# A transformer layer on one core: the residual stream by tokens instead of by features

## The chip, the cores and the metric

The kernel runs on one core of one Trainium2 chip. The metric is the device time of one execution in microseconds. The core has five engines that work side by side: TensorE (PE, the matrix products; its weight loads stand apart as PEld), VectorE (DVE), ScalarE (ACT), GpSimd (POOL) and SyncE (SP, here only the queue of most transfers). A matrix product contracts over the 128 partitions: one operand stands still in the array (the stationary one, up to 128 columns), the other moves through it (up to 512 columns), and the result lands in a bank of PSUM with the stationary operand's columns as its partitions. Everything else works on SBUF or PSUM, 128 partitions at a time.

## The reference

One layer on 512 tokens of width 1024, in fp32. The attention part (two kinds of sparse attention, merged by two sigmoid gates) gives `merged`; the change begins behind it:

```
x = x + merged @ w_out[i]
gate, up = jnp.split(rms_norm(x, g_ffn[i]) @ w_ffn_in[i], 2, axis=-1)
x = x + (jax.nn.silu(gate) * up) @ w_ffn_out[i]
ple_gate = jax.nn.sigmoid(rms_norm(x, g_ple[i]) @ w_ple_gate[i])
x = x + ple_gate * (p[i] @ w_ple_proj[i])
```

`rms_norm` divides each token by the root of the mean square of its 1024 features and multiplies by a gain per feature. The FFN's hidden width is 2816, or 22 tiles of 128. `p` has 512 tokens of width 256.

## The kernel before

**Products.** Every fp32 operand is split into a high and a low part in the matmul's format: ACT copies the high part (`wh`, `x2h`), DVE subtracts it for the low one (`wl`, `x2l`). A product is three matmuls: high by high, high by low, low by high. In `tmm` (L467) the weights stand still and the activations, kept transposed (features on partitions, 512 tokens along the row), move; results come out transposed too.

**The stream.** From the output projection on the residual stream X2 is kept transposed, eight tiles of 128 features by 512 tokens. `w_out` (`wob`, L470-472) makes one feature tile after the other, 24 matmuls each; `residual` (L1066) adds half of it to X2 on DVE, splits it with the gain (L338 on ACT, L339 on DVE) and adds its square to `ssum` (ACT, then POOL). The norm of a token is a sum over partitions, so `rms_stats` (L430) takes it on PE: eight small matmuls with ones (L434, `st1b`), the power -0.5 on POOL (L438), and eight products with a diagonal that spread it over the partitions (L445, `st1c`) into `rb`. It is multiplied in behind the first FFN product.

**The FFN.** The hidden width goes by 22 tiles `m`. The first six are plain (`hidden_plain`): gate `fg` and up `fu`, 24 matmuls of 512 columns each. The others (`hidden_seven`, `seven`) use seven block products in the place of eight, in banks `sa`, `sb`, `sc`, 84 matmuls of 256 columns a tile; the sums of weight blocks that these need are made by POOL's queue with transfers that add in memory (`adding`, L259, two steps of `add` for each pair of blocks and sum), and those of the activations by `normed_blocks` and `Blocks` on DVE. The output product runs three times (`ffn_out`, behind tiles 8, 16 and 21), also by seven block products, with the hidden tiles standing still; so its results have tokens on the partitions. They gather in `acc` (`xn`), added by `into` from banks on DVE (in phase 0 most are first written by copies on ACT).

**The end.** The embedding product (`pj`, 48 matmuls in `pjb`, L1279) stands ahead of the last `ffn_out`. In `turned_back` (L1322) 32 transposes on PE (L1324, `fob`) turn `acc` round, DVE adds X2 (read back from memory, where `kept` holds it since L1298), ACT and DVE split it, and the squares are summed. The gate product (`pg`, 8 output tiles in `pgb`) begins with three tiles on the first four feature tiles, goes on when the upper four are split, and `gated` (L1352) multiplies by `rb2`, takes the tanh, multiplies with the embedding, adds X2 and writes the transposed output, which the host turns.

**Order.** Weights are loaded by SP in the order of a list `units`, into buffers of two tags, `wr` (three) and `wx` (two, L80: the first block "11" of `ffn_out` and half the blocks of a seven-product tile), up to seven ahead, and split into four `wh` and `wl`; each get of one splits the one after next (L128). The instructions are ordered per engine before the run by a scheduler that simulates them; `tc.issue_after` binds one behind another. Engines then run their queues strictly in order.

Of the kernel before, what the change touches and what calls it, by code (L numbers as in the profile page):

```python
# [18 lines left out]
S = 512  # L19
# [6 lines left out]
PLAIN = 6  # L26
# [6 lines left out]
BIG_BUFS = 33  # L33
# [5 lines left out]
OUT_ORDER = [("11", 0), ("11", 1), ("t1", 0), ("t2", 0), ("t1", 1), ("t2", 1), ("21", 0), ("22", 0)]  # L39
OUT_LATE = [[("t3", 0), ("t3", 1), ("21", 1), ("22", 1), ("t4", 0), ("t4", 1)],  # L40
            [("21", 1), ("22", 1), ("t3", 0), ("t3", 1), ("t4", 0), ("t4", 1)]]
# [19 lines left out]
class Weights:  # L61
# [11 lines left out]
    def load(self, upto):  # L73
        while self.n_raw < min(upto, len(self.units)):
# [5 lines left out]
            pool, bufs = (self.pool, 3) if tag == "wr" else (self.more, 2)  # L80
# [20 lines left out]
    def parts(self):  # L101
# [9 lines left out]
        if tag != "wr" and key[0] == "fo":  # L111
            self.kept[key[3]] = t
# [7 lines left out]
        for a, b in self.pieces(i, n):  # L120
            for c, d in self.halves(i, n) if i else [(a, b)]:
                self.nc.scalar.activation(h[:, c:d], t[:, c:d], AF.Copy)  # L122
# [84 lines left out]
def hybrid_kernel(ctx: ExitStack, tc: tile.TileContext, a, out):  # L207
# [45 lines left out]
    for nm, c in (("un", 4), ("wo", 8)):  # L253
        units += [((nm, i), a[nm][i], 1024) for i in range(c)]
# [4 lines left out]
    def adding():  # L259
# [20 lines left out]
        for m in range(0, a["fi7"].shape[2], 4):  # L280
            yield from pair_of_sums(a["fi7"], m, 4, put_fi)
# [20 lines left out]
    def out_units(ph):  # L302

        for name, kp in OUT_ORDER + OUT_LATE[ph == 2]:
# [5 lines left out]
                   "t2": lambda: f"11{kp}", "22": lambda: f"11{kp}"}[name]()  # L310
            yield (("fo", ph, name, f"{name}{kp}"), src, n, "wx" if name == "11" else "wr")
# [28 lines left out]

    ssum = cp.tile([128, 512], F32, name="ssum")

    def add_square(src, first):
        if first:
            A.activation(ssum, src, AF.Square)
        else:
            q = t2("sqx")
            A.activation(q, src, AF.Square)  # L348
            G.tensor_tensor(ssum, ssum, q, op=OP.add)  # L349
# [40 lines left out]
    big_mask = cp.tile([128, 512], F32, name="big_mask")  # L390
# [39 lines left out]
    def rms_stats(name, tags="ss", sums=None):  # L430
        if sums is None:
            sums = bank(name + "b", tags[0])[:, :QT]
            for i in range(QT):
# [1025 lines left out]
```

## Time and profile before

| | us |
|---|---|
| median of 3 runs | 840.03 |
| lowest, highest | 835.34, 840.16 |
| the profiled execution | 834.49 |
| its span | 832.6 |
| PE busy | 815.4 (98%) |
| DVE, ACT, POOL busy | 651.0, 479.6, 173.5 |
| output projection from, to | 384.22, 428.26 |
| plain FFN tiles to | 495.40 |
| last matmul | 827.29 |

The span is that of the profiled instructions; the execution's own time lies 1.9 us above it. In rows of a timeline the first number is the start in the span, the second the duration, then the engine, the line, the result and its sources, and in brackets the idle time of the engine before it with what ended it. Matmuls are pipelined: their durations overlap, so a stage is read from start to start.

### The profile page before, as it was taken

The page shows a single profiled execution, that of the slowest core. Times are in us where ns is not written, and L with a number is a line of the kernel's source. Part 1 is how long each engine was busy: PE and PEld are TensorE (multiplying, and loading weights), DVE is VectorE, ACT ScalarE, POOL GpSimd, SP SyncE. Part 2 cuts the span into 40 slices and gives each one's busy share as a digit, 9 for nine tenths or more (in the row PEclk, how much of TensorE's full clock was granted, in tenths as well). Part 3 has the DMA queues.
Part 4 walks back from the last instruction along what each step waited for, and adds up shares of the span by engine and source line. Part 5 has one row for each costly group of instructions (what it writes and reads, how often), then busy time and mean ns, then how long its engine had stood idle before and what let it go on. Part 6 is the DMA issues. An engine that isn't in the chain of part 4 may idle for free.

```text
span 832.6 us, 12780 instructions
## 1 busy us (share of the span) xinstructions
PE 815.4 (98%) x4653; PEld 712.2 (86%) x4653; DVE 651.0 (78%) x1175; ACT 479.6 (58%) x899; POOL 173.5 (21%) x203
## 2 busy tenths in 40 slices
PE   9999999999999999999999999999999999999897
PEld 8888898788788888787888889789999889988786
DVE  7799677888787987749637988777888977967955
ACT  6455655967676767733433546545666446664531
POOL 3726244010000110106322242000111100200211
PEclk9999999999999999999999999999999999999999
DMA  9443554488664776735442347344445354544402
GB/s 340 145 123 117 154 148 154 127 206 217 187 175 112 203 190 176 184 98 201 165 141 83 106 122 201 113 150 138 138 129 177 100 149 119 153 146 148 149 26 101
DMA packets 39981, 125.13 MB, mean 150 GB/s; under 512 B 5104, under 2 KB 5488, under 8 KB 36464
## 3 DMA queue, kind: packets, MB, share of 16 engines
q1 hardware_dynamic: 34448, 91.82, 34.3%
q0 software_dynamic: 3968, 28.31, 14.3%
q10 hardware_dynamic: 1504, 4.21, 1.6%
q8 instruction: 36, 0.59, 0.3%
q14 instruction: 25, 0.20, 0.1%
HBM read 116.98 MB, written 32.51 MB: 180 GB/s over the span
## 4 chain that ended last, share of the span: by engine, by line
PE 86%; DVE 9%; ACT 2%; issue 1%; DMA 1%; POOL 0%; DVEq 0%; ACTq 0%; POOLq 0%
PE sa L470 4%; PE sa L472 3%; PE sa L471 3%; DVE wl L125 3%; PE ga L470 3%; PE pt L914 3%; PE ga L471 3%; PE ga L472 3%; PE sv L1266 2%; PE sv L1269 2%; PE sv L1268 2%; PE sc L470 2%; PE sc L471 2%; PE sc L472 2%; PE wob L471 2%; PE pv L938 2%
## 5 line engine op out<-in xcount | busy, mean ns | idle before, releaser
L122 ACT ACTIVATE wh<-wr 128x512 fp32r<-128x512 f32 (+2 forms) x243 | 196.2, 828 | 193.8 <-issue 37.4
L125 DVE TENSOR_TENSOR wl<-wr,wh 128x1024 fp32r<-128x1024 f32 (+2 forms) x195 | 229.4, 1180 | 70.7 <-ACT wh L122 69.9
L470 PE MATMUL ga<-xh,wh 128*128 128x512 f32 x128 | 53.5, 418 | 0.0
L889 DVE CUSTOM_DVE_ANT_0 p<-sb,big_mask 128x512 f32<-128x512 f32 (+2 forms) x96 | 44.4, 484 | 9.8 <-PE sb L887 9.5
L471 PE MATMUL ga<-xl,wh 128*128 128x512 f32 x128 | 50.4, 394 | 0.0
L472 PE MATMUL ga<-xh,wl 128*128 128x512 f32 x128 | 50.4, 393 | 0.0
L914 PE MATMUL pt<-ident,p 128*128 128x128 f32 x240 | 38.7, 274 | 1.5 <-DVE pw L924 1.5
L924 DVE TENSOR_TENSOR pw<-pt,pw 128x512 fp32r<-128x512 f32 x48 | 32.6, 683 | 6.0 <-ACT pw L923 5.7
L923 ACT ACTIVATE pw<-pt 128x512 fp32r<-128x512 f32 x48 | 28.1, 593 | 13.3 <-PE pt L914 11.2
L1186 POOL TENSOR_TENSOR hg<-zg,u 128x256 f32<-128x256 f32 x8 | 9.3, 1163 | 126.1 <-ACT zg L1185 126.1
L914 PEld LDWEIGHTS pt<-ident,p 128*128 128x128 f32 x240 | 28.6, 140 | 6.5 <-issue 1.4
L349 POOL TENSOR_TENSOR ssum<-ssum,sqx 128x512 f32<-128x512 f32 x10 | 17.2, 1719 | 70.4 <-ACT sqx L348 70.4
L472 PEld LDWEIGHTS ga<-xh,wl 128*128 128x128 f32 x128 | 24.0, 188 | 5.5
L471 PE MATMUL pgb<-x3l,wh 128*128 128x512 f32 (+1 forms) x72 | 26.5, 371 | 2.1 <-DVE x3l L339 2.1
L1186 POOL TENSOR_TENSOR hf<-zg,u 128x256 f32<-128x256 f32 x8 | 12.9, 1609 | 72.8 <-DVE h L1119 50.4
L115 DVE TENSOR_TENSOR wr<-wr 128x512 f32<-128x512 f32 x32 | 26.2, 818 | 1.8 <-DMA wr<-fi7s 1.2
L471 PEld LDWEIGHTS ga<-xl,wh 128*128 128x128 f32 x128 | 24.2, 189 | 3.1
L470 PEld LDWEIGHTS ga<-xh,wh 128*128 128x128 f32 x128 | 24.2, 189 | 3.0
L472 PE MATMUL pgb<-x3h,wl 128*128 128x512 f32 (+1 forms) x72 | 26.5, 368 | 0.0
L470 PE MATMUL pgb<-x3h,wh 128*128 128x512 f32 (+1 forms) x72 | 25.1, 371 | 0.0
L471 PE MATMUL wob<-ML,wh 128*128 128x512 f32 x64 | 24.9, 392 | 0.2 <-DVE ML L1049 0.2
L470 PE MATMUL wob<-MH,wh 128*128 128x512 f32 x64 | 24.8, 389 | 0.0
(1057 smaller groups left out, 2745.7 us busy)
## 6 DMA issues: line engine op xcount, KB each, us to landing
fi7s<-fi POOLq DMA_DIRECT2D x16, 1024.0 KB, 8.0
wr<-fi SPq DMA_DIRECT2D x48, 256.0 KB, 2.7
wr<-ga SPq DMA_DIRECT2D x16, 512.0 KB, 3.8
fo7s<-fo POOLq DMA_DIRECT2D x8, 1024.0 KB, 7.8
wr<-fi7s SPq DMA_DIRECT2D x32, 256.0 KB, 2.9
wr<-fo SPq DMA_DIRECT2D x15, 512.0 KB, 3.5
wr<-fi SPq DMA_DIRECT2D x12, 512.0 KB, 3.5
wr<-fo7s SPq DMA_DIRECT2D x10, 512.0 KB, 3.5
```

The source lines that it names most:

```text
L115: self.nc.vector.tensor_add(t[:, k:k + 512], self.last[:, :512], self.last[:, 512:])
L122: self.nc.scalar.activation(h[:, c:d], t[:, c:d], AF.Copy)
L125: self.nc.vector.tensor_sub(l[:, a:b], t[:, a:b], h[:, a:b].bitcast(F32))
L349: G.tensor_tensor(ssum, ssum, q, op=OP.add)
L470: T.matmul(o, wh[:, sl], h, start=start, stop=False, skip_group_check=skip)
L471: T.matmul(o, wh[:, sl], l, start=False, stop=False, skip_group_check=skip)
L472: return T.matmul(o, wl[:, sl], h, start=False, stop=stop, skip_group_check=skip).ins
L889: V.tensor_tensor_reduce(out=p, in0=o, in1=big_mask[:, 512 - n:512], op0=OP.add, op1=OP.min, scale=1.0, scalar=3.0e38, accum_out=st["m"][: ...
L914: last = T.transpose(b[:, off:off + 128], st["p"][:, P_OFF[qt] + kb * 128:P_OFF[qt] + kb * 128 + 128], ident)
L923: A.activation(ph, b[:, :off], AF.Copy)
L924: V.tensor_sub(pl, b[:, :off], ph.bitcast(F32))
L1186: on_gpsimd = HI.tensor_tensor(out[:, half(1)], hi, u, op=OP.mult).ins
```

## The change

The stream stays by tokens: X is four token tiles of 128 tokens by 1024 features, read from `xN`, and the output is written so. The output projection, the embedding and the gate product get x as the stationary and the weights as the moving operand (`by_tokens`, `embedding`; the weights' layout is changed on the host). The squares are summed along the row by ACT in the same instruction, and the norm of a token is a number per partition (`square_sums`, `inverse_rms`): no matmul and no spreading. `normed` multiplies X with it, half on ACT and half on DVE, and since the FFN still wants features on partitions, `turned_half` turns the result with 16 transposes for each half of the tokens into banks `yt`, from which ACT and DVE take it times the gain (XF), and split it (x2h, x2l). The embedding product is moved between and behind these transposes; its result goes to memory (`kept`) and comes back as PQ. Four FFN tiles are plain, 18 go by seven products. The norm no longer stands in the hidden tiles; blocks 11, 21 and 22 are parts of x2h themselves (`summed_blocks`). `into` adds into X on DVE in all three phases. The tag `wx` has three buffers; "t2" and "22" are made from two kept weights; the order of blocks in the last `ffn_out` differs. The steps of `add` are 36 in the place of 32 and begin with the fifth hidden tile, not the third. `turned_back` splits straight from PSUM; `gated` has the norm as a scale of ACT's tanh. The removed lines of `rms_stats`, `turned_back` and the gate product stand above and are cut here.

```diff
-PLAIN = 6
+PLAIN = 4
...
-            pool, bufs = (self.pool, 3) if tag == "wr" else (self.more, 2)
+            pool, bufs = (self.pool if tag == "wr" else self.more), 3
...
-            t = self.kept[src]
-            self.nc.vector.tensor_add(t[:, :n], t[:, :n], self.last[:, :n])
+            t, q = (self.kept[x] for x in src.split("+"))
+            self.nc.vector.tensor_add(t[:, :n], t[:, :n], q[:, :n])
...
-    for nm, c in (("un", 4), ("wo", 8)):
+    for nm, c in (("un", 4), ("wo", 8), ("pj", 2)):
...
+                   "t2": lambda: f"11{kp}+t1{kp}", "22": lambda: f"11{kp}+21{kp}"}[name]()
+            yield (("fo", ph, name, f"{name}{kp}"), src, n, "wx" if name == "11" or (ph, name, kp) == (2, "21", 0) else "wr")
...
-        if ph == 2:
-            units += [(("pj", i), a["pj"][i], 1024) for i in range(2)]
...
+    def inverse_rms(sums, rn):
+        V.tensor_scalar(rn, sums, 1.0 / D, EPS, op0=OP.mult, op1=OP.add)
+        G.tensor_tensor(rn, rn, half_neg[:, :rn.shape[1]], op=OP.pow)
...
-    w01 = [W.get(("wo", o)) for o in range(2)]
-    b01 = [bank("wob", "sv"[o]) for o in range(2)]
...
+    pin = t4("pin", F32)
+    nc.sync.dma_start(pin, a["pT"].rearrange("k p t -> p k t"))
+    PIh, PIl = t4("PIh"), t4("PIl")
+    A.activation(PIh, pin, AF.Copy)
+    G.tensor_tensor(PIl, pin, PIh.bitcast(F32), op=OP.subtract)
+    kept = dram.tile([4, 128, 1024], F32, name="kept")
...
+    X = [[t4(f"X{r}{i}", F32) for i in range(2)] for r in range(2)]
+    def tokens(tt, i):
+        return X[tt % 2][i][:, tt // 2]
+    by_half = a["xN"].rearrange("(j r) p c -> r p j c", r=2)
+    for i in range(2):
+        for r in range(2):
+            nc.sync.dma_start(X[r][i], by_half[r][:, :, 512 * i:512 * i + 512])
+    def square_sums(name):
+        parts = cp.tile([128, 2, QT], F32, name=name + "sq")
+        total = cp.tile([128, QT], F32, name=name + "rn")
+        def add(tt, i):
+            A.activation(t2("sqx"), tokens(tt, i), AF.Square, accum_out=parts[:, i, tt:tt + 1])
+        def inverse(t0, t1):
+            r = total[:, t0:t1]
+            V.tensor_add(r, parts[:, 0, t0:t1], parts[:, 1, t0:t1])
+            inverse_rms(r, r)
+            return r
+        return add, inverse
+    def by_tokens(nm, c, banks, h, l, held, halfway=None):
+        def products(tt, kp, wh, wl):
+            for o, cols in banks[tt]:
+                for j in range(2):
+                    kt = 2 * kp + j
+                    w1, w2 = (w[:, 512 * j:512 * j + 512][:, cols] for w in (wh, wl))
+                    T.matmul(o[:, cols], h[kt][:, tts(tt)], w1, start=kt == 0, stop=False)
+                    T.matmul(o[:, cols], h[kt][:, tts(tt)], w2, start=False, stop=False)
+                    T.matmul(o[:, cols], l[kt][:, tts(tt)], w1, start=False, stop=kt == KT - 1)
+        for kp in range(4 - held):
+            w = W.get((nm, 4 * c + kp))
+            for tt in range(QT):
+                products(tt, kp, *w)
+            if halfway and kp == 1:
+                halfway()
+        late = [W.get((nm, 4 * c + kp)) for kp in range(4 - held, 4)]
+        after = None
+        for tt in range(QT):
+            with tc.issue_after(after) if after else nullcontext():
+                for kp, w in enumerate(late, 4 - held):
+                    products(tt, kp, *w)
+            after = yield tt
+    def whole(names):
+        return [[(bank("nt", t), slice(0, 512))] for t in names]
+    add_square, inverse_1 = square_sums("st1")
+    Y = [None] * QT
+    def residual(tt, i, b):
+        t = tokens(tt, i)
+        V.scalar_tensor_tensor(t, b, 0.5, t, op0=OP.mult, op1=OP.add)
+        add_square(tt, i)
+    def normed(tt):
+        r = inverse_1(tt, tt + 1)
+        y = Y[tt] = t4(f"Y{tt}", F32)
+        A.activation(y[:, 0], tokens(tt, 0), AF.Copy, scale=r)
+        V.tensor_scalar(y[:, 1], tokens(tt, 1), r, None, op0=OP.mult)
+    xh, xl = slabs("x2h"), slabs("x2l")
+    XF = [t4(f"XF{j}", F32) for j in range(4)]
+    def turned_half(hf):
+        bs = []
+        for j in range(4):
+            b = bank("yt", "sv"[j % 2])
+            for k in range(2):
+                for r in range(2):
+                    ins = T.transpose(b[:, 256 * k + 128 * r:256 * k + 128 * r + 128],
+                                      Y[2 * hf + r][:, j // 2, tts(2 * (j % 2) + k)], ident).ins
+            bs.append(b)
+        def leave(j):
+            for k in range(2):
+                gain, x = gv[:, 1, 2 * j + k:2 * j + k + 1], XF[j][:, k, half(hf)]
+                if k == 0:
+                    A.activation(x, bs[j][:, half(k)], AF.Copy, scale=gain)
+                else:
+                    V.tensor_scalar(x, bs[j][:, half(k)], gain, None, op0=OP.mult)
+        def split(j):
+            x, h, l = (t[:, :, half(hf)] for t in (XF[j], xh.tile(j), xl.tile(j)))
+            A.activation(h, x, AF.Copy)
+            V.tensor_sub(l, x, h.bitcast(F32))
+        leave(0)
+        for j in range(4):
+            if j < 3:
+                leave(j + 1)
+            split(j)
+        return ins
+    def embedding():
+        ws = [W.get(("pj", kt)) for kt in range(2)]
+        PP = slabs("PP", F32)
+        for n in range(8):
+            tt, c = divmod(n, 2)
+            b = bank("pjb", "aabb"[n % 4])
+            for kt, (wh, wl) in enumerate(ws):
+                w1, w2 = (w[:, 512 * c:512 * c + 512] for w in (wh, wl))
+                T.matmul(b, PIh[:, kt, tts(tt)], w1, start=kt == 0, stop=False)
+                T.matmul(b, PIh[:, kt, tts(tt)], w2, start=False, stop=False)
+                T.matmul(b, PIl[:, kt, tts(tt)], w1, start=False, stop=kt == 1)
+            A.activation(PP[n], b, AF.Copy, scale=0.5)
+            if c:
+                A.dma_start(kept[tt], flat(PP.tile(tt)))
+            yield
+    for tt in by_tokens("wo", 0, (banks := whole("ssvv")), MH, ML, 2):
+        residual(tt, 0, banks[tt][0][0])
+    for tt in by_tokens("wo", 1, (banks := whole("aabb")), MH, ML, 3):
+        residual(tt, 1, banks[tt][0][0])
+        if tt < 3:
+            normed(tt)
+    other = embedding()
+    first_half = turned_half(0)
+    with tc.issue_after(first_half):
+        steps(other, 2)
+    normed(3)
+    with tc.issue_after(first_half):
+        steps(other, 3)
+    with tc.issue_after(turned_half(1)):
+        run(other)
...
-    rb1 = None
     def hidden_plain(m, out):
-        nonlocal rb1
         bg, bu = bank("fg", "a"), bank("fu", "b")
...
+        w = [W.get(("fi", m, i)) for i in range(2)]
+        for b, (wh, wl) in zip((bg, bu), w):
             for kt in range(KT):
...
-        zg, u = t2("zg"), t2("u")
-        V.tensor_tensor(zg, bg, rb1, op=OP.mult)
-        A.activation(zg, zg, AF.Silu, scale=2.0)
-        V.scalar_tensor_tensor(u, bu, 2.0, rb1, op0=OP.mult, op1=OP.mult)
-        return G.tensor_tensor(out, zg, u, op=OP.mult).ins
+                tmm(b, wh, wl, kt, xh[kt], xl[kt], kt == 0, kt == KT - 1)
+        zg = t2("zg")
+        A.activation(zg, bg, AF.Silu)
+        return V.tensor_tensor(out, bu, zg, op=OP.mult).ins
...
+    def summed_blocks(j):
+        x, y = flat(XF[j]), flat(t4(f"ys{j}", F32))
+        b11, b12, b21, b22 = (x[:, half(i)] for i in range(4))
+        t1, t2_, t3, t4_ = (y[:, half(i)] for i in range(4))
+        V.tensor_sub(t1, b11, b12)
+        V.tensor_sub(t3, b22, b12)
+        V.scalar_tensor_tensor(t2_, t1, -1.0, b22, op0=OP.mult, op1=OP.subtract)
+        V.scalar_tensor_tensor(t4_, t2_, -1.0, b21, op0=OP.mult, op1=OP.subtract)
+        XB.split(j, (y, ("t1", "t2", "t3", "t4")))
+        for name, kt, hf in (("11", 2 * j, 0), ("21", 2 * j + 1, 0), ("22", 2 * j + 1, 1)):
+            XB.at[j, name] = xh[kt][:, half(hf)], xl[kt][:, half(hf)]
...
-        if first and name in ("11", "t1", "t2", "t4"):
-            A.activation(to, o, AF.Copy, scale=1.0 if op == OP.add else -1.0)
-        elif name == "11":
+        if name == "11":
             c = t2("fc")
             A.activation(c, o, AF.Copy)
-            V.tensor_tensor(to, to, c, op=op)
-        else:
-            V.tensor_tensor(to, to, o, op=op)
+            o = c
+        V.tensor_tensor(to, to, o, op=op)
...
+            if ph == 2 and name == "t1":
+                turned(W.begun)
...
-            if m < 4:
-                normed_blocks(m)
-            if m == 3:
-                for i in range(4):
-                    A.dma_start(kept[i], flat(X2.tile(i)))
-            if m >= 2:
+            if m < 2:
+                for j in (2 * m, 2 * m + 1):
+                    summed_blocks(j)
+            if m >= PLAIN:
...
+    PP = slabs("PQ", F32)
     for i in range(4):
-        nc.sync.dma_start(flat(X2.tile(i)), kept[i])
+        nc.sync.dma_start(flat(PP.tile(i)), kept[i])
     xh, xl = slabs("x3h"), slabs("x3l")
...
+    add_square, inverse_2 = square_sums("st2")
+    def turned_back(i):
+        for kt in range(4 * i, 4 * i + 4):
+            b = bank("fob", "a")
+            for tt in range(QT):
+                T.transpose(b[:, tts(tt)], tokens(tt, i)[:, tts(kt % 4)], ident)
+            norm_split(b, gv[:, 2, kt:kt + 1], xh[kt], xl[kt])
+        for tt in range(QT):
+            add_square(tt, i)
+    ffn_out(2, lambda: turned_back(0))
+    anchors.clear()
+    rh2 = cp.tile([128, QT], F32, name="st2rh")
 
     def upper():
-        for o in range(4):
...
+        turned_back(1)
+        V.tensor_scalar(rh2, inverse_2(0, QT), 0.5, None, op0=OP.mult)
+    def gated(tt, c, b, cols):
         z, y = t2("pz"), t2("po")
...
+        at = slice(512 * c + cols.start, 512 * c + cols.stop)
+        A.activation(z[:, cols], b[:, cols], AF.Tanh, scale=rh2[:, tt:tt + 1])
+        V.scalar_tensor_tensor(z[:, cols], z[:, cols], 1.0, PP[2 * tt + c][:, cols], op0=OP.add, op1=OP.mult)
+        V.tensor_tensor(y[:, cols], z[:, cols], tokens(tt, c)[:, cols], op=OP.add)
+        nc.sync.dma_start(out[tt][:, at], y[:, cols])
+    banks = whole("ssvv")
+    for tt in by_tokens("pg", 0, banks, xh, xl, 2, upper):
+        gated(tt, 0, *banks[tt][0])
+    banks = whole("aab") + [[(bank("nt", "bs"[i]), half(i)) for i in range(2)]]
+    for tt in by_tokens("pg", 1, banks, xh, xl, 2):
+        for b, cols in banks[tt]:
+            gated(tt, 1, b, cols)
...
```

On PE, the end of the output projection and the first products of the FFN. Before (`wob` the projection's bank, `fg` the gate's, ML and MH the merged attention, the numbers tell buffers apart):

```order
L470 MATMUL wob<-MH_4188,wh_4430 128x512
L471 MATMUL wob<-ML_4190,wh_4430 128x512
L472 MATMUL wob<-MH_4188,wl_4431 128x512
L470 MATMUL fg<-x2h_4267,wh_4469 128x512
L471 MATMUL fg<-x2l_4268,wh_4469 128x512
```

And now, at the first products of the FFN (`pjb` is the embedding's bank, `fu` that of the up product; L1170-1172 and L458-460 are the three matmuls of a product):

```order
L1172 MATMUL pjb<-wh_4397,PIl 128x512
L1170 MATMUL pjb<-wh_4549,PIh 128x512
L1171 MATMUL pjb<-wl_4550,PIh 128x512
L1172 MATMUL pjb<-wh_4549,PIl 128x512
L458 MATMUL fg<-x2h_4529,wh_4555 128x512
L458 MATMUL fu<-x2h_4529,wh_4678 128x512
L458 MATMUL fg<-x2h_4529,wh_4684 128x512
L458 MATMUL fu<-x2h_4529,wh_4762 128x512
L459 MATMUL fg<-x2l_4530,wh_4555 128x512
```

The FFN stood right behind the projection; now the embedding, with the transposes ahead of and between its tiles, lies between them, and four banks are begun with the high part of the first feature tiles before the low part is read.

On ACT, the work behind the output projection. Before (L338 makes x2h from X, L348 the square, L122 a weight's high part; in brackets the semaphores that an instruction waits for):

```order
L122 ACTIVATE wh_4516<-wr_4358 128x1024 [waits DMAHW3_49,PE_49,Activation_49]
L338 ACTIVATE x2h_4462<-X_4202,gv 128x512 [waits DMAHW4_49,DVE_49]
L348 ACTIVATE sqx<-X_4202 128x512 [waits Pool_49]
L122 ACTIVATE wh_4620<-wr_4397 128x1024 [waits DMAHW4_49,PE_49,Activation_49]
L338 ACTIVATE x2h_4462<-X_4202,gv 128x512 [waits DVE_49]
```

And now, the nine rows that end with the split which the first FFN product reads (L1146 takes XF from a transposed bank, L1152 makes x2h, L1173 copies the embedding from its bank, L1175 writes it to memory):

```order
L1152 ACTIVATE x2h_4541<-XF_4213 128x2x256 [waits DVE_49]
L1173 ACTIVATE PP_4610<-pjb 128x512 [waits PE_49]
L1152 ACTIVATE x2h_4545<-XF_4214 128x2x256 [waits DVE_49]
L1146 ACTIVATE XF_4211<-yt,gv 128x256 [waits PE_49]
L1146 ACTIVATE XF_4212<-yt,gv 128x256 [waits PE_49]
L1175 DMA kept<-PP_4610 128x1024 [waits Activation_49]
L1173 ACTIVATE PP_4664<-pjb 128x512 [waits PE_49]
L123 ACTIVATE wh_4684<-wr_4395 128x1024 [waits DMAHW5_49,PE_49]
L1152 ACTIVATE x2h_4529<-XF_4211 128x2x256 [waits DVE_49]
```

Splits of X came one by one beside the projection; now the copies of the embedding, its transfers and a weight's split stand between the splits of the turned tokens.

More of the change, by code (lines that the diff above doesn't have):

```diff
@@ L278, in put_fo @@
             added["sum", *divmod(g, 2), name] = t
-        for m in range(0, a["fi7"].shape[2], 4):
-            yield from pair_of_sums(a["fi7"], m, 4, put_fi)
+        last = a["fi7"].shape[2]
+        for m in range(0, last, 4):
+            yield from pair_of_sums(a["fi7"], m, min(4, last - m), put_fi)
         for g, n in ((0, 2), (2, 2), (4, 1)):
@@ L389, in hybrid_kernel @@
     V.memset(half_neg, -0.5)
-    big_mask = cp.tile([128, 512], F32, name="big_mask")
+    big_mask = pp.tile([128, 512], F32, name="big_mask", tag="big_mask", bufs=1)
     G.memset(big_mask, 0.0)
@@ L1253, in ffn_out @@
         banks = {}
[L1254 removed]
+        for name, kp in OUT_ORDER[ph == 2]:
             tag = place[name]
@@ L1273, in ffn_out @@
                 if kp == 1:
-                    into(name, r, o, ph == 0)
-    PP = slabs("PP", F32)
-    kept = dram.tile([4, 128, 1024], F32, name="kept")
-    def embedding():
-        for i in range(2):
-            wh, wl = W.get(("pj", i))
-            for j in range(4):
-                b = bank("pjb", "ab"[j % 2])
-                for kt in range(2):
-                    ins = tmm(b, wh, wl, 2 * j + kt, PIh[:, kt, :], PIl[:, kt, :], kt == 0, kt == 1)
-                anchors.append(ins)
-                turned(A.activation(PP[4 * i + j], b, AF.Copy, scale=0.5).ins, 4 * i + j == 2)
+                    into(name, r, o)
     m = 0
@@ L1317, in hybrid_kernel @@
     xh, xl = slabs("x3h"), slabs("x3l")
-    upper_sum = cp.tile([128, 512], F32, name="rb", tag="rb", bufs=1)
-    def turned_back(o):
-        b = bank("fob", "a")
-        for t in range(QT):
-            T.transpose(b[:, tts(t)], acc[t % 2][o // 4][:, t // 2, 128 * (o % 4):128 * (o % 4) + 128], ident)
-        t = X2[o]
-        V.tensor_tensor(t, b, t, op=OP.add)
-        norm_split(t, gv[:, 2, o:o + 1], xh[o], xl[o])
-        if o < 4:
-            add_square(t, o == 0)
-        else:
-            q = upper_sum if o == 4 else t2("sqx")
-            A.activation(q, t, AF.Square)
-            if o > 4:
-                V.tensor_add(upper_sum, upper_sum, q)
@@ L1361, in hybrid_kernel @@
-    V.tensor_add(ssum, ssum, upper_sum)
-    rb2, _, _ = rms_stats("st2", "vb")
-    for o in range(8):
-        if o < 3:
-            gated(o, [banks[o]], [slice(0, 512)])
-            continue
-        wh, wl = W.get(("pg", o))
-        cols = [slice(0, 512)] if o < 7 else [half(0), half(1)]
-        bs = [bank("pgb", "ab"[(o + i) % 2]) for i in range(len(cols))]
-        for b, c in zip([*bs], cols):
-            for kt in range(KT):
-                tmm(b[:, c], wh, wl, kt, xh[kt][:, c], xl[kt][:, c], kt == 0, kt == KT - 1)
-        gated(o, bs, cols)
+    add_square, inverse_2 = square_sums("st2")
```

143 lines of the change are left out of this document (29 added, 114 removed), and 3 rows, old and new, of the table OUT_ORDER.

## The prediction

> **What bounds the kernel now.** I read the page from the top first: busy times, then the clock row, then the chain that ended last.
>
> ```profile
> span 832.6 us, 12780 instructions
> PE 815.4 (98%) x4653; PEld 712.2 (86%) x4653; DVE 651.0 (78%) x1175; ACT 479.6 (58%) x899; POOL 173.5 (21%) x203
> ...
> PEclk9999999999999999999999999999999999999999
> ...
> PE 86%; DVE 9%; ACT 2%; issue 1%; DMA 1%; POOL 0%; DVEq 0%; ACTq 0%; POOLq 0%
> ```
>
> TensorE is busy for 98% of the span, at the full granted clock in every slice, and the chain is PE's for 86%. So the time is the number of matmul columns, plus the few places where PE waits. The rest is answered by windows. Each of the following has the columns PE busy, (instructions), clock, DMA share and GB/s; the cuts are at the starts of stages.
>
> ```profile
> 428.26:495.40 67.14, 67.14 (x305) 1.00 0.35 106
> 451.88:495.40 43.52, 43.52 (x193) 1.00 0.38 114
> 566.03:576.11 10.08, 10.08 (x86) 1.00 0.41 122
> 735.79:746.70 10.91, 10.91 (x50) 1.00 0.20 72
> 777.10:827.29 50.19, 48.06 (x251) 1.00 0.21 78
> ```
>
> The second row is four plain FFN tiles, 192 matmuls of 512 columns: 43.52/192 = 226.7 ns each, 10.88 us a tile. The third is one seven-product tile: 84 matmuls of 256 columns in 10.08 us, 120 ns each. The first row holds all six plain tiles and the first norm; the fourth the embedding product, 48 matmuls; the last the gate product and the second norm. The waits of PE behind `uno`, and the borders of the stages, stand in its timeline (start, duration, line, out<-in, and in brackets the idle time before it and what ended it):
>
> ```profile
> 384.22 0.39 PE L470 MATMUL wob<-MH,wh 128*128 128x512 f32 x1
> 428.26 0.39 PE L470 MATMUL fg<-x2h,wh 128*128 128x512 f32 x1
> 526.39 0.38 PE L470 MATMUL sa<-xb0t,wh 128*128 128x256 f32 x1 [2.03 <-ACT u L1181]
> 645.56 0.38 PE L470 MATMUL sa<-xb0t,wh 128*128 128x256 f32 x1 [0.18 <-ACT u L1181]
> 776.31 1.03 PE L1324 MATMUL fob<-ident,xn 128*128 128x128 f32 x8
> 777.10 0.72 PE L470 MATMUL pgb<-x3h,wh 128*128 128x512 f32 x2
> 785.18 0.50 PE L471 MATMUL pgb<-x3l,wh 128*128 128x512 f32 x1 [2.13 <-DVE x3l L339]
> 827.29 0.28 PE L472 MATMUL pgb<-x3h,wl 128*128 128x256 f32 x1
> ```
>
> **The change, part by part.** *Two plain tiles become seven-product tiles:* 2 x (10.88 - 10.08) = **-1.6 us**. The sums of their weights are made by transfers that add in memory, and the DMA share of 0.35 in the plain stage leaves room.
>
> *The first norm leaves PE.* The sums over partitions and their spread go; by tokens a square and its accumulation on ACT give them. 67.14 - 6 x 10.88 = **-1.86 us**, of which the two groups below are 1.68. *The second norm* goes likewise, and with it the wait at 785.18: there X is added, split on ACT, then on DVE, after the last add of the FFN; now the transposed halves are split straight from PSUM, one DVE step shorter, and the cover ahead of their use grows from 36 matmuls to 48. The stage held 50.19; its 168 matmuls at 226.7 ns and 48 at 120 ns are 43.85, its 16 transposes 1.6 (below): 4.7 us over. I take **-4.5**, all but 0.2; if the 2.13 us wait stays, -2.4. DVE's tail work per gate tile falls from three operations to two, and ACT's tanh reads PSUM directly, so neither becomes later.
>
> ```profile
> 436.37 0.79 PE st1b L434 x8
> 444.57 0.89 PE st1c L445 x8
> ```
>
> *The output projection* is 192 matmuls before and after. 428.26 - 384.22 = 44.04 against 43.52: **-0.4** for the waits on MH and ML at its start, since 24 matmuls (four token tiles) now go over two feature tiles of them before the next two are needed, where two output tiles went through six in 36; if they remain, 0. The embedding product (10.91) only moves.
>
> *The stall at 526.* Its cause is ahead of it on ACT: a split of a weight that came late stood in front of the copy of `u`.
>
> ```profile
> 517.78 7.12 DMA wr<-fo
> 525.01 1.06 ACT L122 ACTIVATE wh<-wr 128x1024 fp32r<-128x1024 f32 x1 [2.77 <-DMA wr<-fo]
> ```
>
> That load was issued only when one of two buffers came free; the change gives the tag three. **-2.2** with the 0.18 at 645.56. If the lateness is the transfer itself (7.12 us against the usual 3.5, below), the stall stays: 0.
>
> *32 new transposes* turn the normed tokens for the FFN. Eight take 777.10 - 776.31 = 0.79 us from start to start, so 32 are **+3.2**. That row's durations are longer than its pitch:
>
> ```profile
> L1324 PE MATMUL fob<-ident,xn 128*128 128x128 f32 x32 | 4.6, 272 | 0.0
> wr<-fo SPq DMA_DIRECT2D x15, 512.0 KB, 3.5
> ```
>
> The Trainium skill, page "TensorE: Matmul & The Clock Gate", "Part 4: PE-mode transpose", puts one 128x128 transpose at about 275 ns in a kernel. The duration in the row agrees with that, the pitch of 99 ns does not; by the page the term would be 8.8 us, an estimate from its figure.
>
> *The new hand-over* behind the output projection is what I can least read off. Nothing waits there before: 428.26 has no bracket, since each feature tile was split as it was made. Now the last token tile must be added, squared, raised to its power, scaled, transposed, left from PSUM (XF), and split twice before the first FFN matmul. PE has 32 transposes and the embedding as cover: 3.2 + 10.9 = 14.1 us. I priced ACT's queue, which is in order, from the last projection matmul to the split that the first FFN matmul reads, by these rows:
>
> ```profile
> L348 ACT ACTIVATE sqx<-X 128x512 f32<-128x512 f32 x10 | 6.1, 615 | 0.0
> L1177 ACT ACTIVATE zg<-sa 128x256 f32<-128x256 f32 x16 | 6.2, 385 | 2.0 <-PE sa L472 0.8
> L122 ACT ACTIVATE wh<-wr 128x1024 fp32r<-128x1024 f32 x114 | 120.0, 1058 | 134.3 <-issue 32.8 <-PE sv L1269 13.2 <-PE pgb L471 8.3
> L1068 DVE SCALAR_TENSOR_TENSOR X<-wob,X 128x512 f32<-128x512 f32 x8 | 5.5, 690 | 14.8 <-PE wob L472 14.8
> L125 DVE TENSOR_TENSOR wl<-wr,wh 128x1024 fp32r<-128x1024 f32 x162 | 206.1, 1276 | 63.6 <-ACT wh L122 63.0
> 429.20 0.33 ACTq L1298 DMA_DIRECT2D kept<-X  x1
> 387.49 0.50 PE L471 MATMUL wob<-ML,wh 128*128 128x512 f32 x1 [0.17 <-DVE ML L1049]
> ```
>
> One square, one half of Y, seven splits and seven copies of the embedding are 16 operations of 512 columns, 16 x 0.615 = 9.8 (estimate: split and copy at the square's price); seven XF of 256 columns 2.7; three issues of `kept` 1.0; one weight split 1.06: 14.6 us. It starts after the add, 0.69 + 0.17, so it ends at 15.4 if ACT never idles: a stall of 1.3. I add 0.5 for ACT waiting on the second half's transposes and 0.17 at each of some six hand-offs to and from PE and DVE: **+2.8**. Bounds: 0 if the scheduler's order lets ACT drop the copies behind (PE's banks for them are double), and, if no step of ACT lies beside one of DVE, 15.4 plus DVE's one add, eight XF halves at about 0.4, six splits at 0.69 and two weight splits at 1.28, some 11 us, less 14.1: +12. I take 2.8, since ACT and DVE have separate XF halves (the code gives each one) and so do run beside each other. Queued behind the weight splits on both engines are the FFN's next weights, which then come late by the same 2 or 3 us and not once more.
>
> *FFN to residual.* Adding phase 0 onto X on DVE, as phases 1 and 2 do now, takes eight copies from ACT. DVE has room: in the stage of ffn_out phase 2 it is busy 23.96 of 30.40 us, in the plain stage it was busy 52.45 of 67.10 (columns PE, PEld, DVE, ACT, POOL), and the plain tiles lose two DVE operations by rb. No term.
>
> ```profile
> 428.30:495.40 67.10, 67.10 (x305) 55.81 (x304) 52.45 (x85) 29.36 (x41) 18.61 (x10) 1.00 0.35 106
> 746.70:777.10 30.40, 30.40 (x143) 25.08 (x142) 23.96 (x32) 15.90 (x21) 0.64 (x1) 1.00 0.56 185
> ```
>
> *The queues* passed: ACT's four writes of `kept` move with the embedding (0.33 each, counted); SP's loads of `pT` and X come in the projection stage, where SP waits for no one; POOL's split of the embedding's input, 2.95 us, moves there too, and POOL's power for the norm, 1.04, may queue behind it or behind an add for MH, at most 3 us; the first three token tiles end some 12, 8 and 4 us before the last (18 matmuls each behind them), so only the last tile's power can matter, and by then the split is done.
>
> ```profile
> 438.46 1.04 POOL L438 TENSOR_TENSOR st1rn<-ms__4551,half_neg 128x4 f32<-128x4 f32 x1 [6.03 <-DVE ms__4551 L436]
> 707.05 2.95 POOL L1311 TENSOR_TENSOR PIl<-pin,PIh 128x1024 fp32r<-128x1024 f32 x1 [10.13 <-ACT PIh L1310]
> 827.61 0.42 DVE L1355 TENSOR_TENSOR pz<-pgb,rb 128x256 f32<-128x256 f32 x1 [2.45 <-PE pgb L472]
> ```
>
> *The end:* behind the last matmul the product with rb, the last row here, goes: **-0.5** with its hand-off.
>
> Sum: -1.6 - 1.86 - 4.5 - 0.4 - 2.2 - 0.5 + 3.2 + 2.8 = **-5.1 us**. The profiled execution took 834.49 (span 832.6), 5.5 below the median, 840.03, and near the lowest run, 835.34. It would become 829.4; from the median I forecast **834.9 us**. The runs shown differ by 4.8 us among themselves, as much as the whole term, so I hold 1% (8.4 us) for what a measurement of this kernel surely tells from no change.
>
> **The rivals.** *The hand-over is covered.* No stall at the FFN's start and every saving whole: -5.1 - 2.8 = -7.9, 832.1. For it: 14.1 us of matmuls stand there as cover. Against: ACT's 15.4.
>
> *The stall at 526 stays,* since the transfer is slow and not its buffer: -2.9, 837.1. For it: 7.12 us beside the median of 3.5. Against: it was issued at 517.78, when a buffer came free.
>
> *The hand-over is serial (slower).* ACT's and DVE's parts of the FFN's input alternate, and the cover runs out: a stall of 12 gives -5.1 - 2.8 + 12 = +4.1, 844.1. It decides from a stall of 7.9 on. For it: both engines are in order, and on the ACT queue a weight's split stands ahead of the first input. Against: separate halves.
>
> *Transposes take their duration.* 32 x 0.272 = 8.7 instead of 3.2: +0.4, 840.4. For it: the row's 272 ns. Against it: the eight in 0.79 us. The rule of the page above comes to the same.
>
> *The change doesn't do what it says:* seven-product tiles run 84 matmuls as counted, so only the norms' waits could fail to go (the wait at 785 stays): -3.0, 837.0.
>
> **How the numbers follow.** Chances: forecast 0.49, covered 0.16, stall stays 0.15, waits stay 0.07, serial 0.09, transposes 0.04. The range leaves out the outer tail of serial and takes in the spread of the runs of before: a set of runs that falls as low as 835.34 did puts the forecast at 830.2 and the covered case at 827.4. So 827.4 to 841. Faster by over 1% (below 831.6): by level alone no case, -7.9 being 0.94%; half of the covered case and a third of the forecast's by the runs' spread, 0.08 + 0.16 = 0.24. Slower by over 1%: half of serial and a part of the unknown hand-overs later on, 0.07. Within: 0.69.
>
> **What would show it.** Right: no norm matmuls; the FFN's first matmul with a bracket of 1 to 4 us that names a split on ACT or DVE; 32 transposes in about 3.2 us; no bracket of over 1 us in the first seven-product tiles after phase 0's weights are loaded; the gate product in 45.5 us or so with its transposes. Wrong: a bracket over 8 us at the FFN's start, a granted clock below 1.0 anywhere, or a new wait between a phase of the FFN's output and the tiles after it.

## The result, and the profile after

The changed kernel takes **842.0 us** (median of 20 runs, 837.95 to 845.16) against 836.78 us of the kernel before (20 runs, 834.41 to 841.97): ratio **1.0053**, 95% interval 1.0035 to 1.007. It is slower by about half a per cent, where -5.1 us was forecast, and 842.0 lies just above the range.

Its profiled execution took 844.05 us, 2 us above the median; that of before lay 2.3 us below its own. So the two traces differ by 9.7 us, more than the medians. The head of the page after, with the lines that were shown of before:

```profile
span 842.3 us, 12917 instructions
PE 819.4 (97%) x4725; PEld 718.0 (85%) x4725; DVE 633.1 (75%) x1167; ACT 486.8 (58%) x931; POOL 141.9 (17%) x192
...
PEclk9999999999999999999999999999998999999999
...
PE 82%; DVE 7%; DMA 4%; ACT 3%; issue 1%; POOL 1%; SPq 0%; ACTq 0%; DVEq 0%; POOLq 0%
```

DMA has 4% of the chain where it had 1%, and one slice of the clock row is no longer full. Where that lies is seen from windows of PE cut at the stages (PE busy, clock, DMA share, GB/s). After: output projection, transposes with embedding, plain tiles, seven-product tiles with two output products, and the rest to the last matmul:

```profile
385.74:429.26 43.52, 43.52 (x193) 1.00 0.42 146
429.26:444.94 15.68, 14.69 (x82) 1.00 0.55 201
444.94:489.36 44.42, 43.95 (x192) 1.00 0.33 101
489.36:761.04 271.68, 262.97 (x1850) 0.98 0.53 159
761.04:837.47 76.43, 76.43 (x376) 1.00 0.29 94
```

And the two long stages of before that have not been shown, the seven-product tiles and the rest:

```profile
495.40:735.79 240.39, 238.18 (x1681) 1.00 0.48 143
746.70:827.29 80.59, 78.46 (x391) 1.00 0.34 118
```

The budget of the 9.7 us: the work ahead of the output projection +1.52 (385.74 against 384.22; the work there is nearly the same in both); the projection -0.52; hand-over, embedding and plain tiles 60.10 against 67.14 + 10.91, which is -17.95, of which two tiles fewer are -21.76 and the rest +3.8; the seven-product tiles +31.29, of which two tiles more are +20.16 and **the rest +11.1**; the gate stage -4.16; the end 4.83 against 5.31, -0.48. No term was forecast for the start, which the change hardly touches; of the others all but one came out near their terms. The one is the seven-product tiles. PE's waits in them, from its timeline, and one row of matmuls behind a wait:

```profile
523.48 0.39 PE L460 MATMUL sa<-x2h,wl 128*128 128x256 f32 x1 [2.89 <-DVE wl L126]
607.79 0.39 PE L458 MATMUL sa<-xb0t1h,wh 128*128 128x256 f32 x1 [1.22 <-ACT zg L1262]
631.88 0.58 PE L458 MATMUL sa<-xb0t1h,wh 128*128 128x256 f32 x1 [3.68 <-ACT zg L1262]
632.27 0.42 PE L459 MATMUL sa<-xb0t1l,wh 128*128 128x256 f32 x1
632.48 0.41 PE L460 MATMUL sa<-xb0t1h,wl 128*128 128x256 f32 x1
```

Behind the second long wait the matmuls of 256 columns start 0.21 us apart (632.27 to 632.48), not 0.12: the granted clock is down. Two windows show it, with the same columns as above; the clock stands behind the count:

```profile
524.77:528.18 3.41, 3.27 (x16) 0.50 0.37 136
630.58:637.41 6.83, 5.53 (x26) 0.50 0.52 172
```

Summed over the stage, starts that come later than their usual pitch make 14.1 us, where before had 2.9. Of the 14.1, some 9.8 are late starts and 4.3 slow matmuls. What DVE waited for at the first place, with the load and its neighbour on the queues:

```profile
512.92 0.42 SPq L90 DMA_DIRECT2D wr<-fi7s  x1
513.06 0.85 POOL L272 DMA_DIRECT2D fo7s<-fo  x1
521.59 0.69 DVE L116 TENSOR_TENSOR wr<-wr 128x512 f32<-128x512 f32 x1 [6.81 <-DMA wr<-fi7s]
wr<-fi7s SPq DMA_DIRECT2D x36, 256.0 KB, 2.9
```

A weight load of 256 KB, issued 0.14 us ahead of a 1 MB step of `add`, lands after 8.6 us, where the median of its kind is 2.9. DVE waits 6.81 us for it in its queue, and PE for DVE. (A sum of blocks takes two steps: the first, L270, copies one block, the second, L272, adds the other; this is a second one.) At the other two places DVE waits for a load as well, ACT for DVE, and PE for ACT:

```profile
603.79 0.69 DVE L116 TENSOR_TENSOR wr<-wr 128x512 f32<-128x512 f32 x1 [3.79 <-DMA wr<-fi]
627.88 0.69 DVE L116 TENSOR_TENSOR wr<-wr 128x512 f32<-128x512 f32 x1 [5.17 <-DMA wr<-fi]
```

Again a second step is the neighbour. For the last of the three, the step issued at 617.70 and the load issued 0.62 us behind it:

```profile
fo7s<-fo POOLq DMA_DIRECT2D x1, 512.0 KB, 9.9
wr<-fi SPq DMA_DIRECT2D x1, 256.0 KB, 9.5
```

The load lands 0.2 us behind the step, where the median of its kind is 2.7 us from issue to landing. After the change all twelve steps that are not done in the attention, 7 MB together, are issued between 503 and 664, inside the seven-product tiles; before, the eight such steps began at 469, and three of them lay in the plain tiles.

### The profile page after: what moved, and what is told of

Same layout as the page of the kernel before. It is cut to its first block, busy times and chain, and to the rows that moved or that the text cites. A ratio compares the mean times of both kernels' runs of the same rounds, so it can differ in the third digit from the quotient of the medians.

```text
span 842.3 us, 12917 instructions
## 1 busy us (share of the span) xinstructions
PE 819.4 (97%) x4725; PEld 718.0 (85%) x4725; DVE 633.1 (75%) x1167; ACT 486.8 (58%) x931; POOL 141.9 (17%) x192
## 4 chain that ended last, share of the span: by engine, by line
PE 82%; DVE 7%; DMA 4%; ACT 3%; issue 1%; POOL 1%; SPq 0%; ACTq 0%; DVEq 0%; POOLq 0%
PE sa L458 4%; PE sa L460 4%; PE sa L459 4%; PE nt L1096 3%; PE nt L1095 3%; PE nt L1094 3%; PE ga L458 3%; PE pt L902 3%; PE ga L460 3%; PE ga L459 3%; PE sv L1356 2%; PE sv L1359 2%; PE sv L1358 2%; DVE wl L126 2%; PE sc L459 2%; PE sc L458 2%
## 5 line engine op out<-in xcount | busy, mean ns | idle before, releaser
L123 ACT ACTIVATE wh<-wr 128x512 fp32r<-128x512 f32 (+2 forms) x253 | 200.5, 815 | 181.5 <-issue 23.1
L126 DVE TENSOR_TENSOR wl<-wr,wh 128x1024 fp32r<-128x1024 f32 (+2 forms) x199 | 232.2, 1170 | 64.1 <-ACT wh L123 62.9
L458 PE MATMUL ga<-xh,wh 128*128 128x512 f32 x128 | 53.7, 419 | 0.0
L1275 POOL TENSOR_TENSOR hf<-zg,u 128x256 f32<-128x256 f32 x9 | 14.6, 1617 | 164.9 <-DVE h L1223 147.0
L458 PEld LDWEIGHTS ga<-xh,wh 128*128 128x128 f32 x128 | 24.2, 189 | 3.0
L1094 PE MATMUL nt<-wh,x3h 128*128 128x512 f32 (+1 forms) x72 | 26.2, 369 | 0.0
L1095 PE MATMUL nt<-wl,x3h 128*128 128x512 f32 (+1 forms) x72 | 26.2, 366 | 0.0
L1096 PE MATMUL nt<-wh,ML 128*128 128x512 f32 x64 | 24.9, 389 | 0.0
L1094 PE MATMUL nt<-wh,MH 128*128 128x512 f32 x64 | 24.9, 389 | 0.0
L1095 PE MATMUL nt<-wl,MH 128*128 128x512 f32 x64 | 24.9, 389 | 0.0
L1096 PE MATMUL nt<-wh,x3l 128*128 128x512 f32 (+1 forms) x72 | 24.8, 370 | 0.0
```

The costliest lines, as they stand in the source:

```text
L123: self.begun = self.nc.scalar.activation(h[:, c:d], t[:, c:d], AF.Copy).ins
L126: self.nc.vector.tensor_sub(l[:, a:b], t[:, a:b], h[:, a:b].bitcast(F32))
L458: T.matmul(o, wh[:, sl], h, start=start, stop=False, skip_group_check=skip)
L1094: T.matmul(o[:, cols], h[kt][:, tts(tt)], w1, start=kt == 0, stop=False)
L1095: T.matmul(o[:, cols], h[kt][:, tts(tt)], w2, start=False, stop=False)
L1096: T.matmul(o[:, cols], l[kt][:, tts(tt)], w1, start=False, stop=kt == KT - 1)
```

## The experiments

Theory T1: these transfers make weight loads late. Its rival T2: seven-product tiles, two more of them now, are too short in these buffers for their own loads, whatever runs beside them. First the steps are moved back:

```diff
-            if m >= PLAIN:
+            if m >= 2:
                 with tc.issue_after(last):
                     next(add, None)
```

> The changed kernel with its steps of add issued from the third hidden tile on, as before the change, instead of from the fifth; nothing else differs. In the changed kernel's trace PE loses 14.1 us between the first seven-product tile and the last ffn_out, where the kernel before loses 2.9. Theory T1 (the 1 MB transfers that add in memory now all fall into the seven-product tiles and make weight loads late): two of the twelve steps move into the plain tiles, the first stall (3.2 us at 523 with its slow matmuls) goes or shrinks, the later ones stay: 2 to 5 us less than the changed kernel, about 838. Theory T2 (seven-product tiles with these buffers are too short for their own weight loads, whatever runs beside them): no more than 1 us of difference, about 842.

Measured: 845.13 us, ratio 1.0109 (1.0087 to 1.013). Worse, and not the experiment that was meant: the two steps did not go into the plain tiles. POOL's timeline has them at the start of the program, and PE waits for its first weights:

```profile
3.05 0.75 POOL L270 DMA_DIRECT2D fo7s<-fo  x1
12.11 0.89 POOL L272 DMA_DIRECT2D fo7s<-fo  x1 [8.31 <-DMA fo7s<-fo]
```

```profile
35.92 0.56 PE L448 MATMUL km<-wh,xh 128*128 128x512 f32 x1 [4.52 <-ACT wh L123]
```

Here `issue_after` held a step only behind an instruction of the step's own engine. The product of a plain tile moved from POOL to DVE in the change, so the plain tiles have no instruction on POOL to hang a step behind, and a free step goes first. That is probably why the change lets `add` begin at the first seven-product tile. From the projection's start to the last matmul this kernel takes 446.0 us, against 451.7 after: the stage gained 5.7 and the start lost 6.2.

Then all steps into the attention, whose POOL instructions can hold them:

```diff
                 with tc.issue_after(seen):
                     next(add, None)
+                    if i >= 12:
+                        next(add, None)
```

> The changed kernel with two steps of add for each of the last twelve jobs of the attention, so that all 36 are issued there and none in the FFN. T1: the stalls in the seven-product tiles fall from 14 us to under 3, the attention grows by at most 1 to 2, so 828 to 834. T2: the stalls stay, 840 to 844. A third outcome, the attention growing by 5 us or more, would say that the transfers cost what they cost wherever they stand.

Measured: 836.74 us, ratio 1.0003 (0.9987 to 1.0019). T1 was right about the stalls and wrong about the attention, and the third outcome came as well. The window of the seven-product tiles is without a wait, PE busy in all of it:

```profile
495.97:753.60 257.63, 257.63 (x1849) 1.00 0.43 139
```

271.68 became 257.63, 14.05 us, with the same matmuls; T2 falls. From the projection on it takes 437.66 us, 5.4 less than before. But the projection starts at 392.37, 8.2 us later than before, and most of that is one wait of PE in the attention and the slow matmuls behind it, at a time when several steps were in flight:

```profile
334.84 0.79 PE L921 MATMUL pv<-pw,VN 128*128 128x512 f32 x1 [5.84 <-ACT pw L911]
```

The converse, in the kernel before: `if i < 20` around the step in the attention, and `m >= PLAIN` in the FFN.

> The kernel before with 20 steps of add in the attention and the other 12 from its first seven-product tile (m = 6) on, as many and as placed as in the changed kernel; nothing else differs. T1: stalls of 1.5 to 4 us appear in the seven-product tiles, 3 to 9 us more than before, 840 to 846. T2: no more than 1 us of difference, 836 to 838.

Measured: 839.79 us against 837.08, ratio 1.0046 (1.0028 to 1.0064), +2.7 us, a little under T1's 3 to 9. Its loop ends with tile 16, so the last of the steps is left out, and one block sum lacks its second term; only its time is used. Waits of 1.2 and 2.3 us appear in the seven-product tiles, and 6.2 us are lost there in all:

```profile
593.99 0.39 PE L470 MATMUL sa<-xb0t,wh 128*128 128x256 f32 x1 [1.22 <-ACT zg L1174]
652.75 0.39 PE L470 MATMUL sa<-xb0t,wh 128*128 128x256 f32 x1 [2.34 <-ACT u L1182]
499.35:742.99 243.64, 238.77 (x1681) 1.00 0.54 163
```

So late steps go with a slower old kernel too, but the stage grew by only 3.3 us (243.64 against 240.39), under a third of the 11.1. Nor is it sure that all of that is the steps': the wait of 2.34, ahead of the second output product, is met again below, in a kernel that has no step near it.

Six plain tiles (`PLAIN = 6`, steps from `m >= 4`):

> The changed kernel with six plain tiles as before, which takes four of the 36 steps of add away, the rest from the fifth hidden tile on as now (two of eight then fall into plain tiles). By matmuls alone it is 1.6 us longer. T1: six steps instead of twelve fall into seven-product tiles, so stalls of about 5 to 7 us instead of 14: 835 to 838. T2: with two such tiles less, 14 x 16/18 = 12.5 us of stalls: 841 to 843.

Measured: 834.64 us, ratio 0.9974 (0.9956 to 0.9993). That is just under T1's 835 to 838, and it came about in another way than T1 said, since the edit had the flaw of the first: tiles 4 and 5 are plain here, so two steps went to the program's start, at 3.04 and 10.65 us, and six stayed in the seven-product tiles. The stage loses 0.6 us, not 5 to 7. Twelve steps cost 14 us and six nearly nothing, so it is not so much per step. The sizes differ too: the twelve move 7 MB, these six 2 MB, in steps of 512 and 256 KB. What size does, and what the load that a step meets, was not tested apart.

The steps spread where POOL can hold them, each behind a one-column copy on POOL that reads what the stage just made (`hidden_plain` returns such a copy):

```diff
+    def step_of_add(ins):
+        with tc.issue_after(ins):
+            next(add, None)
+
+    def seen_by_gpsimd(t):
+        return G.tensor_copy(small("seen", [128, 1]), t[:, 0:1]).ins
...
+        if tt == 1:
+            step_of_add(seen_by_gpsimd(tokens(tt, 0)))
...
-            if m >= PLAIN:
-                with tc.issue_after(last):
-                    next(add, None)
+            step_of_add(last)
```

> The changed kernel with its last twelve steps of add issued one at a time from the up projection to the sixth hidden tile (two in the up projection, two in the output projection, two beside the embedding, four in the plain tiles, two in the first seven-product tiles), each behind a small copy on GpSimd that reads what the stage just made. T1: from the output projection's start to the last matmul 437 to 439 us (the kernel before 443.1, the changed kernel 451.7, all steps in the attention 437.7), nothing lost in the seven-product tiles, and no new stall in the attention, so 5 to 6 us below the kernel before: ratio 0.993 to 0.995. T2, or a cost that the transfers have wherever they stand: 3 us or more of new waits in the output projection or the plain tiles, ratio 0.998 or more.

Measured: **828.94 us** (5 runs, 828.15 to 830.12), ratio **0.9902** (0.9884 to 0.992). Its windows from the output projection on:

```profile
384.68:428.20 43.52, 43.52 (x193) 1.00 0.73 229
428.20:443.87 15.67, 14.69 (x82) 1.00 0.69 234
443.87:488.31 44.44, 43.98 (x193) 1.00 0.48 142
488.31:745.94 257.63, 257.63 (x1849) 1.00 0.44 143
745.94:822.37 76.43, 76.43 (x375) 1.00 0.28 94
```

437.69 us together, as with all steps in the attention. The transfers cost nothing in the output projection though the DMA share there rises from 0.42 to 0.73, and the hand-over keeps its length (15.67 us). This version is faster than both kernels. The gain in time, 8 to 9 us, is larger than T1's 5 to 6 and than the 5.4 of its trace against the trace of before, because the trace of before was one of its quicker executions.

The same for the kernel before, with its two buffers of `wx`:

> The kernel before with its last eight steps of add issued likewise from the up projection to the fourth plain tile; two buffers of the tag wx as before. If the stall at 526 came from transfers that add in memory, it goes, though the buffers are still two: 2 to 3 us less than before, ratio 0.996 to 0.998. If it came from the second buffer being freed late, as the prediction has it, the stall of 2 us stays: ratio 0.999 to 1.001.

Measured: 833.78 us, ratio 0.9954 (0.9938 to 0.997), 4.1 us less than before and a little more than expected. The wait at 526 goes though the buffers are two: the output product starts at 526.52, 30.48 us behind the first seven-product tile, where before had 32.52. Another, at the same place ahead of the second output product, which had 0.18 us before, is 2.28 here:

```profile
644.36 1.06 ACT L122 ACTIVATE wh<-wr 128x1024 fp32r<-128x1024 f32 x1 [3.03 <-DMA wr<-fo]
646.26 0.39 PE L470 MATMUL sa<-xb0t,wh 128*128 128x256 f32 x1 [2.28 <-ACT u L1192]
```

No step of `add` is near it. ACT waits for a load of 512 KB that was issued at 637.41 and took 6.9 us, where the same load took 4.7 in the trace of before; why is open. So a load can be late without a step beside it. With three buffers and spread steps (above) neither wait is there, but the third buffer's share was not measured alone. Spread steps in both kernels, side by side on one chip: 828.94 against 833.78, **-4.8 us** (ratio 0.994) for the change itself.

A second trace of the changed kernel:

> The changed kernel once more, unchanged, for a second trace. T1: the same three places (near 523, 607 and 632, shifted by the start of the output projection) hold the stalls again, 10 to 16 us in all with the slow matmuls behind them. If the stalls stand at other places or sum to under 6 us, their place in the first trace was chance.

Measured: 842.96 us; the three places hold again, 13.7 us lost in the stage. At the first, PE now stops some 3 us later, for ACT. At each of the three, the load issued 0.6 us behind a second step takes 11.6, 8.0 and 8.7 us.

```profile
488.65:759.92 271.27, 261.94 (x1849) 0.98 0.52 159
526.86 0.58 PE L458 MATMUL sa<-xb0t1h,wh 128*128 128x256 f32 x1 [4.63 <-ACT zg L1262]
608.87 0.39 PE L458 MATMUL sa<-xb0t1h,wh 128*128 128x256 f32 x1 [1.54 <-ACT zg L1262]
632.39 0.39 PE L458 MATMUL sa<-xb0t1h,wh 128*128 128x256 f32 x1 [3.10 <-ACT zg L1262]
```

The worth of the two tiles by itself (spread steps, `PLAIN = 6`):

> The changed kernel with its steps of add spread as in the best version so far, and six plain tiles as before instead of four. What is left of the change is then all but the two tiles, with nothing stalled behind transfers. The prediction's term for the two tiles says 2 x 0.8 = 1.6 us more than with four: 439.3 from the output projection's start to the last matmul, about 830.5. If the change of tiles was worth nothing beside the rest, it stays at 437.7 and 829.

Measured: 829.53 us, ratio 0.9923 (0.9904 to 0.9942); 439.28 us from the projection to the last matmul against 437.69, +1.59. The term of 1.6 stands in the trace; in time, 829.53 against 828.94 from two sets of runs, it is within what the runs vary.

Last, the slow matmuls:

```diff
+    def gap(k):
+        t = first_of_pair
+        for _ in range(k):
+            u = t2("sqx")
+            G.tensor_copy(u, t)
+            t = u
+        anchors.append(T.transpose(bank("gap", "a")[:, :128], t[:, :128], ident).ins)
```

> The best version so far with TensorE made to wait ahead of hidden tiles 7, 11, 13 and 15 for a chain of 1, 2, 3 and 4 copies on GpSimd (about 1.1 us each), behind the tile before; no transfer is added and the steps of add are long done. Theory C (a wait of PE of over about 3 us lowers its granted clock for some us, whatever it waited for): no slow matmuls behind the first gap, 256-column matmuls at 210 ns instead of 120 behind the gaps of over 3 us, costing 1.2 to 2.5 us each. Theory D (the slow matmuls come with the transfers that add in memory): all matmuls stay at 120 ns, the four gaps alone are lost.

Measured: 864.69 us, in a single run. The gaps did not come out graded: all four are 6.1 to 6.9 us, so the lower end of theory C was not tested by it. Slow matmuls stand behind each of the four, losing 2.3, 1.5, 1.0 and 2.0 us, and the last step of `add` was issued at 511.92, 14.6 us ahead of the first gap's end; theory D falls.

```profile
526.55 0.47 PE L1388 MATMUL gap<-ident,sqx 128*128 128x128 f32 x1 [6.07 <-POOL sqx L1386]
527.26 0.41 PE L460 MATMUL sa<-x2h,wl 128*128 128x256 f32 x1
527.47 0.41 PE L458 MATMUL sa<-x2h,wh 128*128 128x256 f32 x1
527.68 0.41 PE L459 MATMUL sa<-x2l,wh 128*128 128x256 f32 x1
```

## Why the prediction was wrong

**The step that failed** is in the first term, two plain tiles for seven-product ones: "The sums of their weights are made by transfers that add in memory, and the DMA share of 0.35 in the plain stage leaves room." There is room in that stage, as the spread version shows, but the change takes the steps out of it: the diff moves their start from `m >= 2` to the first seven-product tile and adds four steps in the attention, which pushes four others into the FFN. The working looked at the mean share of one stage, put the transfers at nothing, and did not ask beside which loads they now run. The price is +11.1 us in the trace, where -2.2 stood for that stage. With the steps out of the stage and the same matmuls, the 14 us are gone, in two variants (all steps in the attention, and spread). Of the signs that the prediction named for being wrong, one came: a granted clock below 1.0, here 0.98 over the stage.

**The stall at 526** was laid to the second buffer alone. It takes a transfer as well: with the steps out of its way and the buffers still two it is gone (the spread kernel before). In the kernel before, that late load was issued 0.63 us behind a second step of 256 KB. What the third buffer adds is open. The rival that it "stays" named the right agent, the slow transfer, for one wait of 2 us; the change brought that agent into the whole stage.

**The other terms held,** most to a few tenths:

| term | forecast | measured in the traces |
|---|---|---|
| two tiles | -1.6 | -1.59 (six plain, spread) |
| output projection | -0.4 | -0.52 |
| first norm, transposes, hand-over | -1.86 + 3.2 + 2.8 = +4.1 | +3.8 |
| second norm and gate | -4.5 | -4.16 |
| end | -0.5 | -0.48 |
| seven-product tiles | -2.2 | +11.1; with the steps spread 257.63 - 260.55 = -2.9 |

The 16 first transposes run from 429.26 to 430.93, 0.104 us each, the pitch that was taken, not the duration. The hand-over's waits stand where they were put, on the split and on the weight behind it, with 1.0 and 0.5 us in brackets and 2.5 us in all:

```profile
429.26 1.91 PE L1138 MATMUL yt<-ident,Y 128*128 128x128 f32 x16
430.93 0.48 PE L1170 MATMUL pjb<-wh,PIh 128*128 128x512 f32 x1
444.94 0.50 PE L458 MATMUL fg<-x2h,wh 128*128 128x512 f32 x1 [0.99 <-ACT x2h L1152]
446.37 0.49 PE L458 MATMUL fu<-x2h,wh 128*128 128x512 f32 x1 [0.47 <-ACT wh L123]
```

So the serial hand-over, the rival that was to make it slower, did not come; the kernel became slower at a place for which there was no rival. The range's upper end, 841, was not meant to hold such a loss; it left even that rival's 844.1 out. The change stays within 1%, the likeliest of the three outcomes, but on the other side of zero. Without the stalls the sum, -5.1, stands beside -5.4 in the traces (spread steps against the kernel before) and -4.8 in time with the steps spread in both kernels. The two spread traces differ by 7.0 from the projection to the last matmul, but that of the old kernel was its slowest run of nine. That the sum came so near is luck in part: its -2.2 stood for a wait that goes without the change too.

**Not foreseen either:** the time ahead of the output projection differs from trace to trace by 1.5 us where the steps are as handed over (384.22, 385.74, 385.04) and by 2.8 with spread steps (384.68, 383.70 with six plain tiles, 386.46 with the made gaps). And the slow matmuls behind a wait add 4.3 us to 9.8 us of late starts.

## What to carry to other kernels

Where a change removes an instruction, ask what was queued behind it: here a product left POOL, with it the only hook in that stage for background transfers, and they moved to the stage with the tightest loads. The mean DMA share does not price a background transfer; the load that runs beside it, and the in-order queue that waits for that load, do. In this kernel such transfers were free in the output projection and the plain tiles, hung behind an instruction of their own engine.

## What the runs showed of the hardware

**A waiting TensorE comes back slow.** Over all traces here, every matmul that starts 3.05 us or more later than its pitch (3.05, 3.16, 3.26, 3.83, 4.68, 4.79, 6.00, and the four made gaps) is followed by matmuls at 0.21 us for 256 columns, 0.43 for 512, that lose about another 1.0 to 2.5 us; of six from 2.19 to 2.50 us only one is (2.38 in the spread kernel before, 1.2 us lost); from the output projection on, none of those up to 1.7 us. The clock in these stretches is 0.50 in the windows above. A long wait is not all there is to it: in the attention of four of the traces the clock is 0.50 for 3.4 or 6.8 us near 224, behind waits of no more than 0.45 us. In the second trace of the changed kernel:

```profile
223.80:227.10 3.30, 3.30 (x12) 0.50 0.24 72
```

In the first trace the clock is 1.00 there. What brings it down at that place stays open. The Trainium skill, page "TensorE: Matmul & The Clock Gate", section "Part 1: The HAM clock gate", says that an idle window of about 3.4 us puts the array at half its clock until it has been busy for such a window again, and that the window runs freely. The traces agree on the clock, 0.50, and on the repair: the slow stretches last one or two times 3.4 us. They do not agree on the idle time that it takes: four starts that were 2.38 to 3.26 us late, and the place near 224, had less. The pitch here grows by 1.76 (0.12 to 0.21) and 1.9 (0.227 to 0.43), not quite 2. So in this kernel a wait of 4 us costs 5 to 6.5, an estimate from the losses above.

**A transfer that adds in memory is a bad neighbour.** One step of 1 MB stretched a 256 KB load from 2.9 to 8.6 us, and at each of the three stalls the load issued 0.62 us behind a second step took 11.1, 7.6 and 9.5 us and landed 0.2 to 0.4 us behind the step. The mean share of the DMA engines in that stage was only 0.53. Two steps at the program's start went with a wait of 4.5 us of PE for a first weight. In the output projection, at a share of 0.73, loads beside a 1 MB step took up to 13.0 us, and PE did not wait for them.
